# Layer norms' factors and biases on the token-major rows: from GpSimd right behind the norm to VectorE steps spread over the next part

## The chip, the cores and the metric

One NeuronCore of a Trainium2 chip runs the whole program. Time is device microseconds (us) of one execution; a kernel's time is the median of its runs. Five engines run side by side, each with a queue of its own that it works off in order: TensorE (PE in the profile) multiplies and transposes into PSUM, VectorE (DVE), ScalarE (ACT) and GpSimd (POOL) work on rows of 128 partitions, SyncE (SP) issues most loads. They wait for one another through semaphores only.

## The reference, cut to what matters

512 tokens of 1024 features pass two layers of feed-forward, token mixer, feed-forward, and then a second block with a mixer and experts. Each of the six parts of the two layers ends in a layer norm:

```python
for l in range(DEPTH):          # DEPTH = 2
    x = layer_norm(ALPHA * x + 0.5 * swiglu(x, ...), ln_f1_g[l], ln_f1_b[l])    # norm 0
    x = layer_norm(ALPHA * x + token_mixer(x, ...), ln_mix_g[l], ln_mix_b[l])   # norm 1
    x = layer_norm(ALPHA * x + 0.5 * swiglu(x, ...), ln_f2_g[l], ln_f2_b[l])    # norm 2
# layer_norm(x, g, b) = (x - mean) * rsqrt(var + eps) * g + b, over the 1024 features
```

Then `second_block(x)`: an RMS norm, three kinds of mixing, a residual, routed experts.

## The kernel before, in words

**Two forms of x.** The token-major rows are four tiles `self.x[0..3]` of 128 tokens by 1024 features in float32. The products need x feature-major and in two parts, `xh` and `xl` (high digits and the rest), as every product is made of three TensorE passes (`mm3`, lines 219 to 222). A weight is loaded, copied by ScalarE into its high part (line 204), and VectorE subtracts to get the low part (line 205); five buffers hold high parts, five low parts.

**The end of a part** is `down_ln`. The last product is made in two halves of 512 features. In the second half, tile after tile: the last products of tile t, then `ln_z` (VectorE adds the residual and takes statistics, lines 305 and 306); after every second tile `ln_finish` (mean, rsqrt by small VectorE steps, and line 316, which subtracts the mean and multiplies by the inverse deviation in place). At that point the row lacks the factor g and the bias b.

**The two ways on.** `pair_T(p)` makes the feature-major parts of a pair of tiles: 16 transposes by TensorE (line 260), ScalarE applies g and b per feature (line 270, eight instructions of 128x256), and in four chunks of 512 columns VectorE copies to `xh` (line 273) and subtracts to `xl` (line 274). The first products of the next part (`self.head`: the mixer's first projection, two feed-forward columns, or the second block's) are issued between the two pairs: they need the first 256 tokens only. The token-major rows get g and b separately, by `ln_affine` (lines 320 and 321): a multiplication by `gB` and an addition of `bB`, rows of 1024 factors and biases that are the same in all partitions and, but for the last norm, already hold the next residual's ALPHA. GpSimd does both, for each of the four tiles: 8 instructions of 128x1024 per norm. These rows are needed only as the residual at the end of the next part. After norm 0 GpSimd's queue also stores them to `xs` (line 370), because the mixer's attention uses the x buffers as scratch; they come back at line 802.

**The last norm** (layer 1, norm 2; `ln_last`) is followed by the second block. There the rows are squared soon, for the RMS norm's factors (`rms`). `affine(0)` is issued ahead of `pair_T(1)`, `affine(1)` behind it; VectorE takes one tile of the four, GpSimd three.

**The order** of instructions on each engine is set when the program is built, by a scheduler that works with estimated durations; within what data allows, an instruction that comes earlier in the program goes first. `tc.issue_after(i)` places an instruction behind i on i's engine, with no wait.

**The next parts.** The feed-forward (`ffn`) goes over 22 columns f: two weights, 48 products of 128x512, an activation, and a split of the result into `hh` and `hl`. The mixer begins with four projections over the four tiles (`proj_tm` with `out_a`, `out_c`, `out_d`, `out_q`), whose results VectorE rotates (`rope`, lines 445 to 448) and ScalarE copies; `out_d` is woven with the queries and keys of the latent branch.

Of the kernel before, what the change touches and what calls it, by code (L numbers as in the profile page):

```python
# [24 lines left out]
NEG = -1e30  # L25
MLA_SCALE = 96.0 ** -0.5

# column offsets of the constant tables
# [4 lines left out]
# column offsets of the feature-major parameters of a layer  # L33
# [6 lines left out]
# the second block's tables, parameters and rows  # L40
# [15 lines left out]
def bc(ap, axis, n):  # L56
    """A view with a new axis of n equal entries."""
    shape = list(ap.shape)
    return ap.unsqueeze(axis).to_broadcast(shape[:axis] + [n] + shape[axis:])
# [7 lines left out]
def rotate(*steps):  # L67
    """The steps of several parts in turn."""
# [9 lines left out]
def weave(main, side, rate):  # L78
    """Runs main's steps, with rate steps of side to each."""
    due = 0.0  # L80
    for _ in main:
        due += rate
        while due >= 1.0:
            due -= 1.0
            next(side, None)


class Unit:
    """One head's causal attention (to one set of keys)."""
# [30 lines left out]
    def products(self, j, out, start, stop):  # L120
        """out += (vh, vl)^T ph and vh^T pl for the keys of tile j: the two halves' sum is v^T p."""
# [10 lines left out]
class DiffUnit(Unit):  # L132
    """One head's difference of two attentions."""
# [27 lines left out]
class Build:  # L161
    def __init__(self, ctx, tc, a):
# [15 lines left out]
        self.heads, self.head = [], None  # L178
        self.ident = self.const.tile([128, 128], F32, name="ident")
# [7 lines left out]
        # keep where q - k >= 0, else NEG  # L187
# [13 lines left out]
    def split(self, hi, lo, src, eng=None):  # L201
        """hi + lo = src, each with the digits that one pass of the tensor engine carries."""
        nc = self.nc
        first = nc.scalar.activation(hi, src, AF.Copy)  # L204
        (eng or nc.vector).tensor_tensor(lo, src, hi.bitcast(F32), ALU.subtract)  # L205
# [18 lines left out]
    def rsqrt(self, out, src, scale, eps):  # L224
        """out = (scale * src + eps) ** -0.5: a first guess from the exponent's bits, then three steps of Newton's."""
# [22 lines left out]
    def pair_T(self, p, g=None, b=None):  # L248
        """Feature-major parts of tokens 256 p .. 256 p + 255 of self.x (affine in the features if g)."""
# [3 lines left out]
        for cc in range(ND // 2):  # L253
# [20 lines left out]
            nc.vector.tensor_tensor(lo, f3, hi.bitcast(F32), ALU.subtract)  # L274
# [48 lines left out]
    def down_ln(self, nk, lhs, src, l, idx, coef, tail):  # L323
        """x = layer_norm(x + coef * (lhs @ w)), lhs in feature-major parts of nk chunks; src[half, pair] the weight."""
# [4 lines left out]
        if self.ln_last:  # L329
            # the gains of the next norm with these; its factors follow at the products  # L330
            for x in gb:
                self.nc.vector.tensor_tensor(x, x, self.par2[:, Q_MIXG:Q_MIXG + 8], ALU.mult)
        for half in range(2):
# [15 lines left out]
            for t in range(NT):  # L349
# [6 lines left out]
                if half == 1 and t > 1:  # L356
                    if t == 3:
                        if self.heads:
                            self.head = self.heads.pop(0)()
                        if self.ln_last:  # L360
                            self.affine(0)
                    self.pair_T(t - 2, *gb)
        if self.ln_last:
            self.affine(1)
            self.rsx = self.rms(0, 2) + self.rms(2, 2)
            return
        for t in range(NT):
            self.ln_affine(t, self.nc.gpsimd)
            if idx == 0:
                self.nc.gpsimd.dma_start(self.xs[t * 128:t * 128 + 128, :], self.x[t])  # L370

    def affine(self, p):
        for k in range(2):
            self.ln_affine(2 * p + k, self.nc.vector if (p, k) == (1, 0) else self.nc.gpsimd)

    def rms(self, t, n):
        """The factors of rms_norm(x) for the tokens of n tiles."""
# [17 lines left out]
    def ffn_head(self, l, which):  # L395
        """What can be done with the first half of the tokens, while the others are still normalised."""
# [1538 lines left out]
```

## Time and profile before

| | us |
|---|---|
| median of 3 runs (3039.59 to 3042.96) | 3039.92 |
| span of the profiled execution | 3047.0 |
| TensorE busy | 2876.3 |
| VectorE busy | 1694.6 |
| ScalarE busy | 1190.5 |
| GpSimd busy | 467.8 |

The profile is of one execution; its span is 7 us (0.2%) above the median, and the durations below are read from it. Idle and busy times of an engine in a stretch, and TensorE's granted clock there (1.00 is 2.4 GHz, 0.50 is 1.2 GHz), come from the view by stretches; the order of instructions from the timeline of one engine; in brackets behind an instruction stands how long its engine had been idle and what ended that.

### The profile page before, as it was taken

Reading aid. Unit: us, or ns where it says so; the run is one execution under the profiler, and the core shown is the slowest. Engines: PE = TensorE matmul, PEld = TensorE weight load, DVE = VectorE, ACT = ScalarE, POOL = GpSimd, SP = SyncE. Lnnn points to the kernel's source line nnn. Section 1 sums busy time; section 2 is a strip of 40 time slices with the busy share of each in tenths; the row PEclk is TensorE's granted clock in tenths of the full one; section 3 lists DMA queues with packets and bytes.
Section 4 is the critical chain, followed back from the end, with each engine's and each line's share of the span. In section 5 each row is a group of like instructions: output and inputs, shape, how many; then the busy total and the mean of one; then the engine's idle time right before and its main releaser. Section 6 shows DMA issues by size and latency. Waiting matters only on the chain. (4 is left out here: it accounts for less than half of the span.)

```text
span 3047.0 us, 38290 instructions
## 1 busy us (share of the span) xinstructions
PE 2876.3 (94%) x14451; PEld 2325.8 (76%) x14451; DVE 1694.6 (56%) x3183; ACT 1190.5 (39%) x2173; POOL 467.8 (15%) x432
## 2 busy tenths in 40 slices
PE   8999989999989999899998999998999988799787
PEld 7888878777778888788886877777888876567675
DVE  4332375877563332633326587666433258966878
ACT  3222135755432221222212475552322114255575
POOL 0000020222020000200003032202000023723334
PEclk9999989999999999899998999999999999789899
DMA  4222232112522222232223211152322212104796
GB/s 160 97 97 91 78 105 77 53 42 75 194 85 97 97 97 90 80 101 97 93 93 100 82 49 47 48 198 75 105 97 97 97 60 70 46 12 156 271 354 266
DMA packets 95554, 322.20 MB, mean 106 GB/s; under 512 B 11120, under 2 KB 11904, under 8 KB 95360
## 3 DMA queue, kind: packets, MB, share of 16 engines
q1 hardware_dynamic: 85248, 285.91, 27.5%
q0 software_dynamic: 5184, 18.88, 1.7%
q10 hardware_dynamic: 4928, 14.88, 1.4%
q8 instruction: 116, 1.90, 0.3%
q14 instruction: 78, 0.64, 0.1%
HBM read 294.98 MB, written 24.64 MB: 105 GB/s over the span
## 5 line engine op out<-in xcount | busy, mean ns | idle before, releaser
L205 DVE TENSOR_TENSOR lo<-raw,hi 128x1024 fp32r<-128x1024 f32 (+4 forms) x370 | 440.2, 1191 | 702.2 <-ACT hi L204 701.9
L204 ACT ACTIVATE hi<-raw 128x1024 fp32r<-128x1024 f32 (+4 forms) x370 | 380.1, 1032 | 1118.5 <-PE pa L221 300.8
L221 PE MATMUL pa<-xl,hi 128*128 128x512 f32 (+1 forms) x808 | 307.2, 380 | 18.6 <-DVE xl L274 18.5
L320 POOL TENSOR_TENSOR x<-x,gB 128x1024 f32<-128x1024 f32 x23 | 58.9, 2579 | 1709.1 <-PE pa L260 1528.3
L220 PE MATMUL pa<-xh,hi 128*128 128x512 f32 (+1 forms) x808 | 307.3, 381 | 13.1 <-DVE xh L273 13.1
L222 PE MATMUL pa<-xh,lo 128*128 128x512 f32 (+1 forms) x808 | 305.2, 378 | 0.0
L221 PE MATMUL pb<-xl,hi 128*128 128x512 f32 (+1 forms) x784 | 292.3, 373 | 0.0
L220 PE MATMUL pb<-xh,hi 128*128 128x512 f32 (+1 forms) x784 | 291.9, 373 | 0.0
L222 PE MATMUL pb<-xh,lo 128*128 128x512 f32 (+1 forms) x784 | 291.9, 372 | 0.0
L417 DVE TENSOR_TENSOR sg<-sg,pb 128x512 f32<-128x512 f32 x88 | 60.5, 688 | 284.4 <-PE pb L222 276.4
L221 PEld LDWEIGHTS pa<-xl,hi 128*128 128x128 f32 x808 | 156.2, 193 | 48.6 <-DVE xl L274 21.8
L220 PEld LDWEIGHTS pa<-xh,hi 128*128 128x128 f32 x808 | 156.3, 193 | 43.3 <-DVE xh L273 16.1
L222 PE MATMUL pa<-hi,xl 128*128 128x512 f32 (+4 forms) x416 | 158.6, 383 | 22.7 <-DVE xl L274 22.7
L220 PE MATMUL pa<-hi,xh 128*128 128x512 f32 (+4 forms) x416 | 164.9, 399 | 13.0 <-DVE xh L273 10.1
L222 PEld LDWEIGHTS pa<-xh,lo 128*128 128x128 f32 x808 | 156.8, 194 | 26.4
L221 PEld LDWEIGHTS pb<-xl,hi 128*128 128x128 f32 x784 | 150.5, 192 | 25.0
L220 PEld LDWEIGHTS pb<-xh,hi 128*128 128x128 f32 x784 | 150.2, 192 | 25.0
L222 PEld LDWEIGHTS pb<-xh,lo 128*128 128x128 f32 x784 | 150.1, 191 | 24.9
L220 PE MATMUL pa<-hi,hh 128*128 128x512 f32 x416 | 165.8, 399 | 1.5 <-ACT hh L204 1.5
L221 PE MATMUL pa<-lo,xh 128*128 128x512 f32 (+4 forms) x416 | 157.5, 379 | 9.4 <-DVE lo L205 9.4
L221 PE MATMUL pa<-lo,hh 128*128 128x512 f32 x416 | 164.7, 396 | 0.1
L222 PE MATMUL pa<-hi,hl 128*128 128x512 f32 x416 | 164.5, 395 | 0.0
(550 smaller groups left out, 6284.4 us busy)
## 6 DMA issues: line engine op xcount, KB each, us to landing
raw<-in_gu SPq DMA_DIRECT2D x176, 512.0 KB, 3.3
raw<-in_wd SPq DMA_DIRECT2D x88, 512.0 KB, 3.3
mraw<-in_eg SPq DMA_DIRECT2D x51, 512.0 KB, 8.4
raw<-in_win_g SPq DMA_DIRECT2D x32, 512.0 KB, 3.2
mraw<-in_ed SPq DMA_DIRECT2D x20, 512.0 KB, 5.3
sig<-sg SPq DMA_DIRECT2D x32, 256.0 KB, 2.0
raw<-in_wp SPq DMA_DIRECT2D x16, 512.0 KB, 4.4
sg<-sig SPq DMA_DIRECT2D x32, 256.0 KB, 3.4
```

The source lines that it names most:

```text
L204: first = nc.scalar.activation(hi, src, AF.Copy)
L205: (eng or nc.vector).tensor_tensor(lo, src, hi.bitcast(F32), ALU.subtract)
L220: nc.tensor.matmul(out, sh, mh, start=start, stop=False)
L221: nc.tensor.matmul(out, sh, ml, start=False, stop=False)
L222: nc.tensor.matmul(out, sl, mh, start=False, stop=stop)
L320: eng.tensor_tensor(self.x[t], self.x[t], self.gB, ALU.mult)
L417: nc.vector.tensor_tensor(sg, sg, pu, ALU.mult)
```

## The change

The factor and bias of a norm leave GpSimd and the end of the part. For five of the six norms they become a sequence of eight VectorE steps (`late_affine`: for each tile the multiplication, then the addition). The mixer takes one step at the end of each `out_c` and one inside each `out_d`; the feed-forward takes one step per column from f = 4 on. What is left is run before the fourth projection, or before the feed-forward's `down_ln`. Each step is placed behind `self.pin`, the VectorE instruction that the program issued last among the subtractions of `split` and `pair_T` and the last sums of `rope`. The stores to `xs` after norm 0 stay in GpSimd's queue and follow their tile's addition. For the last norm, each `pair_T` is followed at once by the four VectorE instructions of its two tiles, placed behind the pair's last subtraction.

```diff
     def split(self, hi, lo, src, eng=None):
         first = nc.scalar.activation(hi, src, AF.Copy)
-        (eng or nc.vector).tensor_tensor(lo, src, hi.bitcast(F32), ALU.subtract)
+        last = (eng or nc.vector).tensor_tensor(lo, src, hi.bitcast(F32), ALU.subtract)
+        if eng is None:
+            self.pin = last
...
@@ pair_T
-            nc.vector.tensor_tensor(lo, f3, hi.bitcast(F32), ALU.subtract)
+            self.pin = nc.vector.tensor_tensor(lo, f3, hi.bitcast(F32), ALU.subtract)
...
@@ down_ln
                 if half == 1 and t > 1:
-                    if t == 3:
-                        if self.heads:
-                            self.head = self.heads.pop(0)()
-                        if self.ln_last:
-                            self.affine(0)
+                    if t == 3 and self.heads:
+                        self.head = self.heads.pop(0)()
                     self.pair_T(t - 2, *gb)
+                    if self.ln_last:
+                        with self.tc.issue_after(self.pin.ins):
+                            for k in range(2):
+                                self.ln_affine(2 * t - 4 + k, self.nc.vector)
         if self.ln_last:
-            self.affine(1)
             self.rsx = self.rms(0, 2) + self.rms(2, 2)
             return
+        self.late = self.late_affine(self.x, self.gB, self.bB, idx == 0)
+
+    def late_affine(self, x, g, b, store):
+        nc = self.nc
         for t in range(NT):
-            self.ln_affine(t, self.nc.gpsimd)
-            if idx == 0:
-                self.nc.gpsimd.dma_start(self.xs[t * 128:t * 128 + 128, :], self.x[t])
+            for y, op in ((g, ALU.mult), (b, ALU.add)):
+                with self.tc.issue_after(self.pin.ins):
+                    nc.vector.tensor_tensor(x[t], x[t], y, op)
+                if store and op == ALU.add:
+                    nc.gpsimd.dma_start(self.xs[t * 128:t * 128 + 128, :], x[t])
+                yield
...
@@ ffn, in the loop over f and behind it
                 act(f, pg, pu)
+                if f > 3:
+                    next(self.late, None)
+            run(self.late)
@@ rope
-        nc.vector.tensor_tensor(dst, t1, t2, ALU.add)
+        self.pin = nc.vector.tensor_tensor(dst, t1, t2, ALU.add)
@@ mixer_, out_c (at its end) and out_d (behind its rope)
+            next(self.late, None)
@@ mixer_, before the fourth projection
+        run(self.late)
```

## Rows read from the trace of the kernel before

**Rows 1.** Page, part 1: busy time, share of the span and instructions of each engine

```profile
PE 2876.3 (94%) x14451; PEld 2325.8 (76%) x14451; DVE 1694.6 (56%) x3183; ACT 1190.5 (39%) x2173; POOL 467.8 (15%) x432
```

**Rows 2.** Waits of TensorE, whole span: who waited for whom, total us, times, longest

```profile
PE pa L220 <- DVE xh L273: 23.2, 22, 1.7
PE pa L222 <- DVE xl L274: 22.7, 11, 5.1
...
PE pa L221 <- DVE xl L274: 18.5, 10, 2.4
```

**Rows 3.** VectorE's timeline, first norm, first pair: start, us, engine, line, operation

```profile
377.97 2.60 DVE L273 CAST xh<-full 128x512 fp32r<-128x512 f32 x1
380.61 2.74 DVE L274 TENSOR_TENSOR xl<-full,xh 128x512 fp32r<-128x512 f32 x1
...
388.54 0.45 DVE L273 CAST xh<-full 128x512 fp32r<-128x512 f32 x1
389.03 0.69 DVE L274 TENSOR_TENSOR xl<-full,xh 128x512 fp32r<-128x512 f32 x1
```

**Rows 4.** GpSimd's timeline in the same stretch; each row merges two instructions

```profile
377.90 4.90 POOL L320 TENSOR_TENSOR x<-x,gB 128x1024 f32<-128x1024 f32 x2 [376.25 <-PE pa L260]
382.75 5.32 POOL L321 TENSOR_TENSOR x<-x,bB 128x1024 f32<-128x1024 f32 x2
```

**Rows 5.** By stretches: from:to, length, busy PE, PEld, DVE, ACT, POOL, clock, DMA

```profile
376.00:400.00 24.00, 17.92 (x71) 14.51 (x70) 21.67 (x33) 6.25 (x11) 11.74 (x10) 0.79 0.45 152
400.00:424.00 24.00, 18.18 (x80) 14.85 (x79) 17.44 (x28) 8.70 (x20) 11.62 (x6) 0.79 0.16 56
848.00:870.00 22.00, 18.00 (x110) 16.02 (x109) 21.15 (x30) 7.26 (x12) 10.58 (x4) 0.92 0.14 49
872.00:894.00 22.00, 15.65 (x101) 14.30 (x100) 14.88 (x11) 7.77 (x13) 10.53 (x4) 0.77 0.23 83
1236.00:1258.00 22.00, 16.26 (x101) 14.82 (x99) 20.93 (x29) 6.44 (x11) 10.15 (x4) 0.84 0.14 48
1260.00:1282.00 22.00, 16.11 (x92) 14.67 (x90) 15.19 (x13) 7.94 (x13) 10.52 (x4) 0.69 0.15 52
1622.00:1646.00 24.00, 17.96 (x71) 14.58 (x72) 21.97 (x33) 6.25 (x11) 11.57 (x10) 0.79 0.47 151
1646.00:1670.00 24.00, 18.20 (x81) 14.87 (x80) 17.43 (x28) 8.70 (x20) 11.59 (x6) 0.79 0.16 56
2099.00:2119.00 20.00, 16.63 (x94) 14.76 (x92) 19.38 (x27) 6.11 (x10) 10.46 (x4) 0.83 0.16 53
2123.00:2143.00 20.00, 13.64 (x85) 12.29 (x84) 13.94 (x10) 7.38 (x13) 10.53 (x4) 0.74 0.23 79
2484.00:2508.00 24.00, 16.90 (x95) 14.98 (x94) 22.91 (x33) 6.01 (x11) 13.01 (x9) 0.79 0.24 73
2508.00:2528.00 20.00, 14.52 (x105) 14.06 (x104) 16.57 (x40) 11.00 (x21) 5.59 (x2) 0.83 0.08 26
```

**Rows 6.** TensorE's timeline: the first product of the mixer's head

```profile
381.20 0.37 PE L220 MATMUL pa<-hi,xh 128*128 128x440 f32 x1
```

**Rows 7.** The one addition of a bias that VectorE makes today, by its line

```profile
L321 DVE TENSOR_TENSOR x<-x,bB x1: 1211/1211/1211, 2519.5 to 2519.5; 128x1024 f32<-128x1024 f32 x1
```

**Rows 8.** By stretches: a feed-forward, and the mixer's third and fourth projection

```profile
910.00:1110.00 200.00, 200.00 (x884) 165.62 (x883) 68.11 (x74) 57.54 (x73) 0.00 (x0) 1.00 0.29 98
464.00:480.00 16.00, 15.46 (x91) 13.65 (x90) 14.27 (x44) 13.40 (x29) 0.00 (x0) 1.00 0.25 82
```

**Rows 9.** VectorE's timeline in the mixer, behind the second projection

```profile
459.21 0.96 DVE L205 TENSOR_TENSOR lo<-raw,hi 128x768 fp32r<-128x768 f32 x1 [8.74 <-ACT hi L204]
```

**Rows 10.** ScalarE's timeline: the attention's first write to a buffer of x

```profile
511.27 0.37 ACT L493 ACTIVATE pr<-pa,sm 128x128 f32<-128x128 f32 x1
```

**Rows 11.** GpSimd's and VectorE's timelines behind the last norm's first pair

```profile
2496.86 2.07 POOL L1184 MEMSET sc<- 128x2048 f32 x1
...
2497.23 0.69 DVE L274 TENSOR_TENSOR xl<-full,xh 128x512 fp32r<-128x512 f32 x1
2497.84 1.38 DVE L273 CAST xh<-full 128x512 fp32r<-128x512 f32 x1
```

More of the change, by code (lines that the diff above doesn't have):

```diff
@@ L178, in __init__ @@
         self.heads, self.head = [], None
+        self.late = iter(())
         self.ident = self.const.tile([128, 128], F32, name="ident")
@@ L356, in down_ln @@
                 if half == 1 and t > 1:
-                    if t == 3:
-                        if self.heads:
-                            self.head = self.heads.pop(0)()
-                        if self.ln_last:
-                            self.affine(0)
+                    if t == 3 and self.heads:
+                        self.head = self.heads.pop(0)()
                     self.pair_T(t - 2, *gb)
+                    if self.ln_last:
+                        with self.tc.issue_after(self.pin.ins):
+                            for k in range(2):
+                                self.ln_affine(2 * t - 4 + k, self.nc.vector)
         if self.ln_last:
-            self.affine(1)
             self.rsx = self.rms(0, 2) + self.rms(2, 2)
             return
+        self.late = self.late_affine(self.x, self.gB, self.bB, idx == 0)
+    def late_affine(self, x, g, b, store):
+        nc = self.nc
         for t in range(NT):
-            self.ln_affine(t, self.nc.gpsimd)
-            if idx == 0:
-                self.nc.gpsimd.dma_start(self.xs[t * 128:t * 128 + 128, :], self.x[t])
-    def affine(self, p):
-        for k in range(2):
-            self.ln_affine(2 * p + k, self.nc.vector if (p, k) == (1, 0) else self.nc.gpsimd)
+            for y, op in ((g, ALU.mult), (b, ALU.add)):
[4 more added lines that the diff above has]
+                yield
     def rms(self, t, n):
@@ L634, in out_d @@
             self.rope(ksw[1][:, t, :, :16], v[:, 1, :, :16], 2, 8, tab(C_NCOS, t, 16), tab(C_NSIN, t, 16))
+            next(self.late, None)
             nc.scalar.activation(ksw[1][:, t, :, 16:], v[:, 1, :, 16:], AF.Copy)
```

## The prediction

> **What bounds the kernel now.** I read the page first: TensorE is busy for 2876.3 of 3047.0 us [rows 1], so what counts is what stops it. The list of its waits comes next. Three lines at its top name one place, the copy and the subtraction that make `xh` and `xl` behind a norm: 23.2 + 22.7 + 18.5 = 64.4 us [rows 2]. Six norms have two pairs of tiles each, so that is some 5.4 us a pair. Third, the timelines of VectorE and GpSimd side by side. In the first pair of the first norm a copy takes 2.60 us and a subtraction 2.74 [rows 3]; in the same pair, once GpSimd has finished at 388.07, they take 0.45 and 0.69 [rows 3, 4]. The long ones start and end with GpSimd's instructions of 2.45 to 2.66 us (4.90 and 5.32 for two) [rows 4]: each VectorE instruction waits until one of GpSimd's is through, then does its own work. Without them a chunk costs 0.45 + 0.69 = 1.14 us instead of 2.60 + 2.74 = 5.34. GpSimd's four instructions hold up two chunks in each pair, so the price is 2 x 4.2 = 8.4 us of VectorE time per pair, on TensorE's path.
>
> The Trainium skill states this as a lock (SBUF — State Buffer, section "SBUF: two separate sides"): VectorE and GpSimd share a pair of ports, the first to start keeps it for its whole instruction, and a VectorE instruction with two SBUF inputs is held only by a GpSimd instruction that reads SBUF. The rows agree, and I use the second half of the rule below.
>
> **What the stalls cost in full.** Fourth, the stretches. Behind every pair TensorE's granted clock falls from its higher level (2.4 GHz) to the lower (1.2 GHz), after it has stood idle for some of the time; the means over such a stretch are 0.69 to 0.92 [rows 5]. What a stretch loses is its length less busy time times clock. For the first pairs of the six norms: 24 - 17.92 x 0.79 = 9.8, and likewise 5.4, 8.3, 9.8, 6.2, 10.7; for the second pairs 9.6, 10.0, 10.9, 9.6, 9.9, 8.0 [rows 5]. Sum: 50.2 + 58.0 = 108.2 us. Of it 268.0 - 200.0 = 68.0 is idle time and 40.2 the slower clock, so a microsecond of such stalls has cost 108.2 / 68.0 = 1.59. The 108.2 are the most that this place can give.
>
> **Removed: 46 GpSimd instructions and their lock.** Not all of the 108.2 returns, since the chain behind the norm remains. First pairs: VectorE starts at 377.97 [rows 3], and at 1.14 us a chunk would be done at 382.5; TensorE arrives at 381.20 [rows 6], when two chunks are ready, and needs the rest one after the other. So a wait of 0 to 1.3 us remains; then come the subtractions of the head's last weights, which VectorE now reaches 8 us earlier. Second pairs: nothing lies between the transposes and the products that need them; TensorE waits for the first chunk and then follows at about VectorE's pace, 0.4 to 2.3 us (a first copy, to half of 4 x 1.14). I take 1 us for each of the 12 pairs, near the middle of both bounds: 12 us remain, 96.2 return, the clock's part with them, because I expect no idle time above 1 us in one piece. Bounds: 80 (2.3 us for each of 12) to 106.
>
> **Added: 46 VectorE instructions of 1.21 us** (the addition that VectorE makes today takes 1211 ns [rows 7]), 55.7 us, at three kinds of place.
>
> *Feed-forward, 3 x 8 steps, 29 us.* VectorE is busy for 68.11 of 200 us there, and TensorE for 200.00 at full clock [rows 8]. A step stands at a column's end, behind its last subtraction; queued behind it are the next weights' subtractions, which run several weights ahead of the products, and the next activation. The cover is VectorE's idle 66%. Cost 0; 29 if the cover were gone. A new wait: the next norm's factors overwrite `gB` and `bB`, so their loads, in ScalarE's queue, now wait for the last of the eight steps; ScalarE's weight copies queue behind, with as much lead. Cost 0, too: those rows are used only a hundred or more us later.
>
> *Mixers, 2 x 8 steps, 9.7 us each.* Here VectorE is not free. Four steps stand in `out_c`. The other four are placed behind the rotations of `out_d`, and VectorE comes to these only after a subtraction for which it stood idle for 8.74 us, at 459.21 [rows 9]: the steps cannot use that gap and land in 464 to 480, where VectorE is busy for 14.27 of 16 us and TensorE already loses 0.54 [rows 8]. Behind each of these steps queue the rotations, the weights' subtractions and the compression's inputs, and TensorE waits for them. There is room for 1.73 us; 4 x 1.21 = 4.84 come. So 3.1 us stick out, and I add 0.4 for the first four: 3.5 a mixer, 7 us in all. Bounds: 0 (the scheduler orders around them) to 2 x 9.7 = 19.4. The `xs` stores move with the additions in GpSimd's queue, which has nothing else to do there; the attention's first write to a buffer of x is at 511.27 [rows 10], some 30 us after the last step. Cost 0.
>
> *Last norm, 8 instructions where VectorE had 2.* Four follow the first pair at once: 4.84 us on VectorE ahead of the head weights' subtractions, of `ln_z` and of the second pair's norm, all of which TensorE needs soon. GpSimd's memsets (the longest 2.07 us [rows 11]), which stand behind its affine instructions today, may come earlier and meet this pair. Cost 5 us, between 0 (ordered behind the urgent ones) and 4.84 + 2.07 = 6.9. In today's trace a memset let a subtraction pass at 0.69 and held a copy for about 1 us (1.38) [rows 11]. By the skill's rule on instructions that read SBUF (same section) a memset could hold only the copies, as these rows have it; by that the upper end stays 6.9. Behind the second pair TensorE has two tiles' products and half a column's, so 1.5 of the 4.84 us, between 0 and 4.84. Together 6.5.
>
> **The sum.** 108.2 - 12 - 7 - 6.5 = 82.7 us. Against the profiled span: 3047.0 - 82.7 = 2964. The median lies 7.1 us (0.23%) below that span, so 3039.9 - 82.7 = 2957 us.
>
> **Rivals.**
> 1. *Everything is hidden.* The scheduler places all steps in gaps, and half a microsecond remains per pair: 108.2 - 6 = 102, 2938 us. For it: VectorE is idle for 44% of the span [rows 1]. Against: the program's order goes first, and the mixer's steps are behind busy rotations.
> 2. *VectorE becomes the bound where the steps stand close.* All 16 steps of the mixers reach TensorE, with the clock: 19.4 x 1.59 = 31; the last norm's first pair returns nothing (9.7) and its second loses 4.8: 108.2 - 12 - 31 - 14.5 = 51, 2989 us. For it: 14.27 of 16 [rows 8]. Against: TensorE has products in store from other branches there.
> 3. *The clock falls anyhow*, at the smaller gaps and the transposes. Only idle time returns: 68.0 - 12 - 13.5 = 42.5, 2997 us. Against: the clock was 1.00 in 464 to 480 with 0.54 us idle [rows 8].
> 4. *Every step stops TensorE (the slower side).* Place: the split behind each step, in feed-forward, mixer and last norm. Price: 48 x 1.21 x 1.59 = 92 against 96 returned, 3036 us; from 2.0 us a step (96 / 48) it is slower, at 2.2 by 9 us, 3049. Against: 200.00 of 200 with a VectorE two thirds idle [rows 8].
> 5. *The change does not do what it says:* the long copies are not GpSimd's doing. Nothing returns, 13.5 are added: 3053 us. Against: 2.60 and 0.45 within one pair, on either side of 388.07 [rows 3, 4].
>
> **How the numbers follow.** Forecast 0.62 (its own range 2945 to 2975: mixers 0 to 14, remainders 6 to 18), rival 1 0.13, rival 2 0.13, rival 3 0.07, rival 4 0.03, rival 5 0.02. Predicted is 2957. The range runs from 2937, which takes in rival 1, to 2989, which takes in rival 2; outside are rivals 3 to 5 and strays, below 2 in 10. A measurement of this kernel tells 0.2% (6 us) from no change: faster is the forecast with rivals 1 to 3, 0.95; same is a part of rival 4, 0.02; slower the rest, 0.03.
>
> **What would show it.** In the trace after: copies at about 0.45 and subtractions at 0.69 behind every norm, no GpSimd instruction beside them; the three waits of [rows 2] from 64 us down to about 10; the clock at 1.00 through the stretches of [rows 5], but for the last norm's; lines of 1.21 us on VectorE in the feed-forwards with TensorE still without a wait; in the mixers new TensorE waits of 2 to 4 us for rotations or weights' low parts after the second projection. It would be wrong if the waits for `xl` stay at 2 us a piece (rivals 3, 5), if the mixers lose more than 10 us (rival 2), or if the feed-forward shows any TensorE wait (rival 4).

## The result and the profile after

| | before | after |
|---|---|---|
| median, us | 3041.44 (3039.59 to 3045.24, 4 runs) | 2956.49 (2947.45 to 2959.41, 4 runs) |
| ratio, 95% interval | | 0.9709 [0.9691, 0.9727] |
| span of the profiled execution, us | 3047.0 | 2945.7 |
| VectorE busy, us | 1694.6 | 1647.5 |
| GpSimd busy, us | 467.8 | 349.0 |

The change makes the kernel 85 us (2.9%) faster. The profiled execution of after is the shortest of its four and that of before lies above all of its runs, so the two pages are 101 us apart. Where a few us matter below, several profiled executions stand side by side.

**VectorE got 46 instructions more and is busy for less time.** Part 1 of the page after answers to [rows 1]: busy time, share of the span, instructions.

```profile
PE 2831.6 (96%) x14451; PEld 2294.7 (78%) x14451; DVE 1647.5 (56%) x3229; ACT 1192.5 (40%) x2174; POOL 349.0 (12%) x386
```

The new instructions add 46 x 1.22 = 56 us and the sum still falls by 47: about 103 us of VectorE's busy time before were time in which an instruction was held, not worked on. VectorE's timeline after, first norm, first pair, answers to [rows 3]:

```profile
377.71 0.43 DVE L276 CAST xh<-full 128x512 fp32r<-128x512 f32 x1
378.18 0.69 DVE L277 TENSOR_TENSOR xl<-full,xh 128x512 fp32r<-128x512 f32 x1
378.79 0.42 DVE L276 CAST xh<-full 128x512 fp32r<-128x512 f32 x1
379.24 0.69 DVE L277 TENSOR_TENSOR xl<-full,xh 128x512 fp32r<-128x512 f32 x1
379.85 0.42 DVE L276 CAST xh<-full 128x512 fp32r<-128x512 f32 x1
```

The first copy took 2.60 us before and takes 0.43, the first subtraction 2.74 and 0.69. Of the 48 copies behind the norms the longest is now 0.46. TensorE's waits after (who waited for whom, total, times, longest) answer to [rows 2]:

```profile
PE pb L1224 <- DVE lvB L1211: 14.6, 3, 11.4
PE pb L1224 <- DVE sm L235: 9.3, 1, 9.3
...
PE pb L1014 <- DVE sm L1013: 4.2, 1, 4.2
...
PE pa L223 <- DVE xh L276: 2.5, 6, 0.7
```

Of the three lines with 64.4 us one is left, with 2.5. The two that lead the list now belong to the second block (`L1224` was `L1210`); they come up again below. The stretches behind the norms, and a feed-forward and a piece of a mixer at the end, answer to [rows 5] and [rows 8]; from:to, length, busy PE, PEld, DVE, ACT, POOL, clock, DMA:

```profile
376.00:391.00 15.00, 14.96 (x79) 13.11 (x77) 13.04 (x33) 6.26 (x11) 0.35 (x4) 1.00 0.52 173
391.00:414.00 23.00, 21.83 (x120) 19.64 (x121) 17.40 (x66) 10.79 (x29) 0.00 (x0) 1.00 0.23 69
829.00:848.00 19.00, 19.00 (x139) 17.89 (x138) 14.96 (x31) 7.77 (x12) 0.00 (x0) 1.00 0.33 111
848.00:868.00 20.00, 19.69 (x140) 18.29 (x139) 11.60 (x16) 12.25 (x18) 0.00 (x0) 1.00 0.32 104
...
2389.00:2408.00 19.00, 16.18 (x112) 14.30 (x110) 17.82 (x37) 5.91 (x11) 2.87 (x5) 1.00 0.33 95
2408.00:2428.00 20.00, 15.05 (x100) 13.89 (x99) 17.85 (x48) 14.02 (x25) 0.00 (x0) 0.83 0.20 64
886.00:1086.00 200.00, 200.00 (x883) 165.48 (x882) 76.88 (x81) 59.63 (x75) 0.00 (x0) 1.00 0.32 103
440.00:460.00 20.00, 19.91 (x114) 17.56 (x113) 18.31 (x55) 14.91 (x31) 0.53 (x1) 1.00 0.39 132
```

Behind five norms TensorE's clock stays at its higher level (1.00), and the ten pairs together lose 3.3 us (the four of the first two norms 0.04, 1.17, 0 and 0.31). In the feed-forward VectorE's busy time rose from 68.11 to 76.88, and TensorE is still busy for 200.00 of 200. Only the last norm still loses time: 19 - 16.18 = 2.8 and 20 - 15.05 x 0.83 = 7.5 us.

**Where the time came from, part by part.** From the first copy behind one norm to the first copy behind the next, each read from VectorE's timeline; the last column goes to the end of the span. `same_again` and `third_look` are further executions of the changed kernel, `before_again` is one of the kernel before.

| us from norm to norm | 0 to 1 (mixer) | 1 to 2 (ffn) | 2 to 3 (ffn) | 3 to 4 (mixer) | 4 to 5 (ffn) | 5 to end |
|---|---|---|---|---|---|---|
| before | 472.1 | 386.6 | 387.6 | 475.1 | 386.6 | 560.9 |
| before_again | 470.3 | 386.8 | 387.6 | 471.1 | 387.0 | 556.5 |
| after | 453.0 | 370.7 | 368.4 | 450.5 | 370.8 | 554.6 |
| same_again | 455.3 | 370.7 | 368.4 | 454.4 | 370.7 | 559.7 |
| third_look | 450.9 | 370.7 | 368.4 | 451.4 | 370.7 | 563.0 |
| saved, of means | 18.1 | 16.0 | 19.2 | 21.0 | 16.1 | -0.4 |
| lost before by [rows 5] | 19.4 | 15.4 | 19.2 | 19.4 | 16.1 | 18.7 |

The first five columns give back what [rows 5] says was lost there: 90.4 against 89.5. By the stretches alone it would be 86.2, as 3.3 us are still lost in them; the other 4 us lie mostly in the second mixer's column, whose executions spread by as much. The sixth column gives back nothing that shows in a spread of 8 us. That is the finding which the experiments had to explain.

### The profile page after: what moved, and what is told of

The parts are those of the page before. It is cut to its first block, busy times and chain, and to the rows that moved or that the text cites. A ratio compares the mean times of both kernels' runs of the same rounds, so it can differ in the third digit from the quotient of the medians.

```text
span 2945.7 us, 38251 instructions
## 1 busy us (share of the span) xinstructions
PE 2831.6 (96%) x14451; PEld 2294.7 (78%) x14451; DVE 1647.5 (56%) x3229; ACT 1192.5 (40%) x2174; POOL 349.0 (12%) x386
## 5 line engine op out<-in xcount | busy, mean ns | idle before, releaser
L225 PEld LDWEIGHTS pb<-xh,lo 128*128 128x128 f32 x784 | 147.8, 189 | 25.5 <-DVE lo L206 0.4
L224 PEld LDWEIGHTS pb<-xl,hi 128*128 128x128 f32 x784 | 147.6, 188 | 24.9
L223 PE MATMUL pa<-hi,xh 128*128 128x512 f32 (+4 forms) x416 | 155.9, 377 | 2.7 <-DVE xh L276 1.5
L224 PE MATMUL pa<-lo,xh 128*128 128x512 f32 (+4 forms) x416 | 151.1, 364 | 6.4 <-DVE lo L206 6.3
L225 PE MATMUL pa<-hi,xl 128*128 128x512 f32 (+4 forms) x416 | 149.3, 361 | 0.0
```

The source lines that it names most:

```text
L223: nc.tensor.matmul(out, sh, mh, start=start, stop=False)
L224: nc.tensor.matmul(out, sh, ml, start=False, stop=False)
L225: nc.tensor.matmul(out, sl, mh, start=False, stop=stop)
```

## The experiments

My theory was the prediction's: GpSimd's instructions hold VectorE's, so the place of the work counts, and the steps cost next to nothing where they stand. The rivals were that the gain comes from the faster engine, or from the work as such, and that the last norm's eight instructions take back more than counted.

**same_again and third_look: the changed kernel again**, for the spread and as neighbours of the others on their chips.

> The changed kernel once more, for a second profiled execution. The changed kernel's four runs lay between 2947.5 and 2959.4 us, with mean granted clocks of 0.974 down to 0.968. If the difference between its executions is the clock in parts that the change does not touch (attention, second block), this execution shows the same intervals from norm to norm within 1 us in the feed-forwards, and differs only where the clock is below 1.00 without idle time. If it comes from the moved steps, the intervals of feed-forward or mixer differ.

> The changed kernel beside the three others of this call, on the same chip: 2950 to 2959 us, and a third profiled execution. From norm to norm its feed-forwards take 352 us again; the stretches with attention and the second block differ by up to 5 us each, with the clock.

Measured: 2954.15 us, 0.9703 [0.9683, 0.9722], and 2953.89 us, 0.97 [0.9686, 0.9714]. The feed-forwards repeat to 0.1 us, the mixers and the second block do not (table above). The 352 us of the second expectation and of a later one, and the 361 to 363 for the kernel before, are counted from a norm's second pair on: 370.7 - 18.8 = 351.9.

**no_affine: what the 48 instructions cost where they now stand.**

```diff
@@ down_ln
                     if self.ln_last:
-                        with self.tc.issue_after(self.pin.ins):
-                            for k in range(2):
-                                self.ln_affine(2 * t - 4 + k, self.nc.vector)
+                        pass
@@ late_affine
-                with self.tc.issue_after(self.pin.ins):
-                    nc.vector.tensor_tensor(x[t], x[t], y, op)
```

> Leaves out the token-major rows' factors and biases altogether (all 48 instructions; the stores stay where they are), so its difference from the changed kernel is the price of the 48 VectorE instructions. Theory (the 40 steps in the next parts are free, the 8 behind the last norm are not): the changed kernel's profile has 2.9 us of TensorE idle time in the last norm's first pair and 7.3 us of idle and slow clock in its second, so some 9 us: 2947 us against 2956. Rival (the steps also cost TensorE time in mixer and feed-forward, 3.5 us a mixer and more): 2940 or less. Second rival (nothing costs anything): within 3 us of 2956.

Measured: 2945.81 us, 0.9679 [0.966, 0.9698], some 8 us below the changed kernel beside it. The five parts up to the last norm's first copy take 2017.9 us (378.04 to 2395.95) against 2013.3, 2019.5 and 2012.2 in the three executions of the table, with the same feed-forwards to 0.1 us: the 40 steps cost nothing that shows. From the last norm to the end it takes 546.9 against 554.6 to 563.0. What the change costs, it costs behind the last norm, with the eight instructions there.

**right_behind: VectorE does the work, but at once behind each pair, at every norm.**

```diff
-                    if self.ln_last:
-                        with self.tc.issue_after(self.pin.ins):
-                            for k in range(2):
-                                self.ln_affine(2 * t - 4 + k, self.nc.vector)
+                    with self.tc.issue_after(self.pin.ins):
+                        for k in range(2):
+                            self.ln_affine(2 * t - 4 + k, self.nc.vector)
+                    if idx == 0:
+                        for u in (2 * t - 4, 2 * t - 3):
+                            self.nc.gpsimd.dma_start(self.xs[u * 128:u * 128 + 128, :], self.x[u])
...
-        self.late = self.late_affine(self.x, self.gB, self.bB, idx == 0)
```

> VectorE does the multiplication and addition of both tiles right behind each pair's last subtraction, for all six norms, as the changed kernel does for the last one only; GpSimd has none of them. Theory (engine and place both count: no lock, but 4.84 us of VectorE work between the pair and what TensorE needs next): each of the ten pairs that change loses about what the last norm's first pair loses today, 2.9 us, so some 29 us: about 2985 us; copies stay at 0.43 us. Rival (only the engine counts, the place is indifferent): 2956. Other rival (only the place counts, work right behind the norm costs the same whoever does it): about 3040.

Measured: 2973.98 us, 0.9772 [0.9756, 0.9788]: 18 to 20 us above the changed kernel. So VectorE in GpSimd's stead gives most of the gain (68 of 88 us), although its work still stands at the norm, and the later place gives the rest, less than the 29 us I expected. (The place is not quite GpSimd's: VectorE's four instructions come behind the pair's last subtraction, GpSimd's ran beside the copies.) VectorE's timeline behind the first pair, and a TensorE wait that comes of it:

```profile
382.03 2.35 DVE L323 TENSOR_TENSOR x<-x,gB 128x1024 f32<-128x1024 f32 x2
384.30 2.35 DVE L324 TENSOR_TENSOR x<-x,bB 128x1024 f32<-128x1024 f32 x2
387.18 1.06 DVE L206 TENSOR_TENSOR lo<-raw,hi 128x880 fp32r<-128x880 f32 x1
```

```profile
388.29 0.47 PE L224 MATMUL pa<-lo,xh 128*128 128x440 f32 x1 [2.37 <-DVE lo L206]
```

The first of these splits of the head's weights starts 9.9 us behind the first copy, against 5.3 in the changed kernel, and TensorE waits 2.4 us for the low part.

**no_pin: the same steps without the fixed point behind `self.pin`.**

```diff
-                with self.tc.issue_after(self.pin.ins):
-                    nc.vector.tensor_tensor(x[t], x[t], y, op)
+                nc.vector.tensor_tensor(x[t], x[t], y, op)
```

> The changed kernel with the 40 late steps placed by program order alone, without the fixed point behind the last subtraction or rotation. Theory (the scheduler takes what is ready: the rows and factors are ready at the norm, so the steps go into VectorE's first gaps, between the norm and the first rotations): the steps move forward into the stretch right behind the pairs, and the time lies near the kernel that does them there, 2965 to 2975 us. Rival (program order keeps them late, the fixed point changes nothing): 2955.

Measured: 2975.07 us, 0.9777 [0.9762, 0.9792], as much as `right_behind`. The scheduler moves the steps forward, since their data are ready; its VectorE timeline:

```profile
378.00 1.23 DVE L377 TENSOR_TENSOR x<-x,gB 128x1024 f32<-128x1024 f32 x1
379.14 0.76 DVE L276 CAST xh<-full 128x512 fp32r<-128x512 f32 x2
...
390.49 1.22 DVE L377 TENSOR_TENSOR x<-x,bB 128x1024 f32<-128x1024 f32 x1
```

The first step stands ahead of the first copy, although the program has it a mixer's projection later. Writing a step later in the program does not place it; the 20 us of the later place come from the line that fixes it.

**pool_late: GpSimd does the work at the late places.** A copy of one column (`o`) of what `self.pin` wrote was meant to hold GpSimd back until then.

```diff
-                with self.tc.issue_after(self.pin.ins):
-                    nc.vector.tensor_tensor(x[t], x[t], y, op)
...
+                nc.gpsimd.tensor_copy(self.seen, o)
+                nc.gpsimd.tensor_tensor(x[t], x[t], y, op)
```

> GpSimd does the late steps at the changed kernel's places in feed-forward and mixer (a small copy of one column of the result that VectorE has just written, about 0.15 us, holds GpSimd until that point); the last norm is as in the changed kernel. Theory (a VectorE instruction meeting one of GpSimd's waits up to 2.6 us, and that costs only where VectorE has no lead): feed-forwards as in the changed kernel, no TensorE wait; in the mixers, where VectorE is busy for 18.3 of 20 us, each of the 8 steps holds it for up to 2.6 us, up to 20 us a mixer: between 2960 and 2990 us. Rival (GpSimd's work costs wherever it runs): about 3040. Second rival (place is all): 2956.

Measured: 3038.58 us, 0.9978 [0.9966, 0.9991]. The experiment did not do what it was to do, as GpSimd's timeline shows:

```profile
377.95 4.90 POOL L383 TENSOR_TENSOR x<-x,gB 128x1024 f32<-128x1024 f32 x2 [376.30 <-PE pa L264]
382.81 5.32 POOL L383 TENSOR_TENSOR x<-x,bB 128x1024 f32<-128x1024 f32 x2
...
437.69 0.19 POOL L382 COPY seen<-ks 128x1 f32<-128x1 f32 x1 [24.75 <-DVE ks L463]
```

Only the copies were held; the scheduler took the work itself ahead of them, back to its old place (compare [rows 4]). It tells nothing of late GpSimd steps. It shows by accident that the changed program with GpSimd right behind the five norms has nearly the old time.

**pool_held: the same, with each step placed behind its copy.**

```diff
-                nc.gpsimd.tensor_copy(self.seen, o)
-                nc.gpsimd.tensor_tensor(x[t], x[t], y, op)
+                seen = nc.gpsimd.tensor_copy(self.seen, o)
+                with self.tc.issue_after(seen.ins):
+                    nc.gpsimd.tensor_tensor(x[t], x[t], y, op)
```

> As the run before it with GpSimd's late steps (there the scheduler had moved GpSimd's instructions back to right behind the norm, since only VectorE's queue had a fixed point), but each multiplication and addition is now placed behind the small copy that holds GpSimd at the changed kernel's place. Theory (the harm is VectorE meeting GpSimd where it has no lead): feed-forward intervals of 352 us as in the changed kernel, tails without a stall, mixers up to 20 us longer each: 2960 to 2990 us. Rival (GpSimd's work costs wherever it runs): about 3040.

Measured: 2963.82 us, 0.9743 [0.9728, 0.9758]. The slow engine at a good place is within 10 us of the changed kernel, better than the fast engine right behind the norm (2974). From norm to norm it takes 456.4, 370.7, 368.4, 457.3 and 370.7: the feed-forwards are those of the changed kernel to 0.1 us, and the mixers lose some 3 and 5. Why, the timelines of GpSimd and VectorE in the first mixer show:

```profile
419.99 2.40 POOL L384 TENSOR_TENSOR x<-x,gB 128x1024 f32<-128x1024 f32 x1
...
432.33 2.41 POOL L384 TENSOR_TENSOR x<-x,gB 128x1024 f32<-128x1024 f32 x1
```

```profile
419.58 0.19 DVE L464 TENSOR_TENSOR ks<-r,r 128x32 f32<-128x32 f32 x1
...
420.09 2.34 DVE L464 TENSOR_TENSOR kc_tm<-r,r 128x32 f32<-128x32 f32 x1
...
432.21 2.59 DVE L464 TENSOR_TENSOR kc_tm<-r,r 128x32 f32<-128x32 f32 x1
```

A sum of 32 columns that takes 0.19 us takes 2.34 and 2.59 beside GpSimd's multiplications and ends within 0.1 us of them. (The second is recorded as starting 0.12 us ahead of GpSimd's; so close a start doesn't settle which came first.) TensorE is busy for 18.09 of the 20 us from 440 on, where the changed kernel has 19.91. This is the hold of [rows 3] at another place and on another instruction; in a feed-forward GpSimd's step of 2.4 us falls into 3.6 us in which VectorE is idle.

**half_pool: the kernel before without the additions of the biases.** Half of GpSimd's work goes; the place and the engine stay.

```diff
         eng.tensor_tensor(self.x[t], self.x[t], self.gB, ALU.mult)
-        eng.tensor_tensor(self.x[t], self.x[t], self.bB, ALU.add)
```

> The kernel before, leaving out the biases' additions on the token-major rows (line 321, 24 instructions), so that GpSimd has two instructions behind each pair instead of four. Theory (each of GpSimd's instructions holds one of VectorE's for its rest): one chunk of each pair is held instead of two, 4.2 us less per pair on VectorE; TensorE's stall falls from some 9 us a pair to 3 or 4, the more as shorter gaps may leave the clock at its upper level: 2970 to 2995 us. Rival (the copies and subtractions are slow for another reason): 3040, with copies still at 2.6 us in two chunks of each pair.

Measured: 2994.57 us, 0.9851 [0.9829, 0.9874], 48 us below the kernel before beside it (3042.94): half the hold gives a little over half of the 85 to 91 us. VectorE and GpSimd in its first pair:

```profile
377.66 2.62 DVE L273 CAST xh<-full 128x512 fp32r<-128x512 f32 x1
380.31 2.74 DVE L274 TENSOR_TENSOR xl<-full,xh 128x512 fp32r<-128x512 f32 x1
382.97 0.46 DVE L273 CAST xh<-full 128x512 fp32r<-128x512 f32 x1
383.47 0.69 DVE L274 TENSOR_TENSOR xl<-full,xh 128x512 fp32r<-128x512 f32 x1
```

```profile
377.59 4.91 POOL L320 TENSOR_TENSOR x<-x,gB 128x1024 f32<-128x1024 f32 x2 [375.95 <-PE pa L260]
```

Two GpSimd instructions hold two of VectorE's, one chunk; the second chunk is short as soon as GpSimd has ended (377.59 + 4.91 = 382.50). In the kernel before it was held too, here its copy:

```profile
383.27 2.59 DVE L273 CAST xh<-full 128x512 fp32r<-128x512 f32 x1
```

So it is GpSimd's instructions that hold VectorE, one by one, which settles rival 5. The Trainium skill's rule (SBUF — State Buffer, "SBUF: two separate sides"), that the loser of the shared pair of ports waits for the other's whole instruction, agrees with these rows and with those of `pool_held`.

**last_as_before: the changed kernel, but the last norm as it was** (`affine(0)` ahead of `pair_T(1)`, `affine(1)` behind it; three tiles by GpSimd).

```diff
...
+                        if self.ln_last:
+                            self.affine(0)
                     self.pair_T(t - 2, *gb)
-                    if self.ln_last:
-                        with self.tc.issue_after(self.pin.ins):
-                            for k in range(2):
-                                self.ln_affine(2 * t - 4 + k, self.nc.vector)
         if self.ln_last:
+            self.affine(1)
...
```

> The changed kernel with the last norm's rows as in the kernel before (GpSimd three tiles, VectorE one). Theory (the last norm gave 6.7 us from its first to its second pair and about nothing behind, since the second pair's stall of 5 us became a wait of 4.2 us for the factors): 6 to 8 us slower than the changed kernel, 2960 to 2964 us; first to second pair 24.9 us again. Rival (the last norm gave the 10 us that were predicted for it): 2965 or more.

Measured: 2955.53 us, 0.9709 [0.9696, 0.9722], against 2953.89 for the changed kernel beside it. My expectation was wrong: with the last norm undone, the time is the same within the intervals. The hold is back, as its VectorE timeline and its stretch show, and still it costs nothing at the end:

```profile
2395.18 2.61 DVE L276 CAST xh<-full 128x512 fp32r<-128x512 f32 x1
```

```profile
2394.00:2418.00 24.00, 16.35 (x85) 14.32 (x84) 22.89 (x32) 6.01 (x11) 12.75 (x9) 0.72 0.23 75
2418.00:2440.00 22.00, 16.52 (x115) 15.84 (x114) 17.21 (x42) 11.59 (x22) 5.59 (x2) 0.84 0.12 42
```

These two lose 12.2 and 8.1 us, the changed kernel's two 2.8 and 7.5: a gain of 10 behind the norm. How far it lasts is seen on VectorE's timeline further on, as time since the last norm's first copy:

| us since the first copy | first scan of decays | first norm of the convolution (`sq`) | last level's sum (`acc`) | end |
|---|---|---|---|---|
| before, before_again | 58.2, 58.6 | 84.8, 85.2 | 201.0, 201.2 | 560.9, 556.5 |
| last_as_before | 59.7 | 88.0 | 200.9 | 558.4 |
| after, same_again, third_look | 48.4, 48.8, 48.3 | 80.5, 80.9, 81.9 | 197.6, 197.6, 198.7 | 554.6, 559.7, 563.0 |
| half_pool | 52.7 | 79.3 | 193.9 | 553.8 |
| no_affine | 41.7 | 68.4 | 182.9 | 546.9 |

A gain of 10 us at the scan is 4 at the convolution's norm and 3 at the last level, and then is lost in a spread of 8 us between executions of one kernel. It need not be so: `half_pool` and `no_affine` come to the scan 6 and 17 us earlier than the kernel before and to the last level 7 and 18 us earlier. From the scan to the last level's sum, by stretches, before, after and `no_affine`:

```profile
2544.00:2688.00 144.00, 116.03 (x1277) 88.01 (x1276) 128.91 (x286) 38.45 (x59) 81.21 (x62) 0.87 0.16 49
2439.00:2589.00 150.00, 118.01 (x1285) 89.67 (x1285) 129.65 (x285) 41.46 (x61) 79.78 (x62) 0.89 0.14 43
2437.00:2579.00 142.00, 115.77 (x1272) 86.88 (x1271) 127.62 (x283) 38.49 (x59) 81.79 (x62) 0.89 0.16 49
```

After takes 6 us longer than before. VectorE is busy there for 0.7 us more and idle for 20.4 us instead of 15.1; most of the added idle time is waits for TensorE ahead of the levels' sums (`tm`: 9.7 us instead of 6.3). And the work has another order: between the scan and the convolution's norm VectorE does eight steps of the convolution's sum (`y<-z,par,y`) in all executions of the changed kernel, and four in `before`, `last_as_before`, `half_pool` and `no_affine`. Inside this stretch lies a piece in which VectorE and GpSimd are both busy almost throughout, first of before, then of after:

```profile
2576.00:2636.00 60.00, 38.66 (x390) 27.96 (x389) 59.77 (x107) 10.12 (x17) 60.00 (x48) 0.77 0.11 36
```

```profile
2481.00:2541.00 60.00, 32.18 (x351) 23.10 (x349) 59.87 (x106) 10.48 (x18) 58.45 (x47) 0.77 0.11 36
```

VectorE is busy for 59.8 of 60 us, GpSimd for 58.5 to 60 and TensorE for 32 to 39: in this piece TensorE is not the bound. VectorE's and GpSimd's timelines in it, of after:

```profile
2481.53 0.15 DVE L237 SCALAR_TENSOR_TENSOR sm<-sm 128x8 f32<-128x8 f32 x1
2481.65 1.07 DVE L1055 SCALAR_TENSOR_TENSOR y<-z,par,y 128x512 f32<-128x512 f32 x1
2482.64 1.22 DVE L235 TENSOR_TENSOR sm<-sm 128x8 f32<-128x8 f32 x1
```

```profile
2482.15 1.69 POOL L1058 TENSOR_TENSOR y<-y,zw 128x512 f32<-128x512 f32 x1
```

An instruction on 8 columns takes 0.15 us or 1.22, and the long one ends (2483.86) with GpSimd's (2483.84). It is the same hold, in a part whose instructions the change doesn't touch. But it doesn't explain the lost gain: before has the same piece, and so has `no_affine`, whose 17 us come through it. Where the changed kernel loses its 10 us is read from the landmarks; that the other order is the reason is not shown, as no run changed the order alone.

**last_later: the last norm's first four instructions behind the head's last weight split.**

```diff
+                        if self.ln_last:
+                            with self.tc.issue_after(self.pin.ins):
+                                for k in range(2):
+                                    self.ln_affine(k, self.nc.vector)
                     self.pair_T(t - 2, *gb)
-                    if self.ln_last:
+                    if self.ln_last and t == 3:
                         with self.tc.issue_after(self.pin.ins):
                             for k in range(2):
-                                self.ln_affine(2 * t - 4 + k, self.nc.vector)
+                                self.ln_affine(2 + k, self.nc.vector)
```

> The changed kernel with the last norm's first four VectorE instructions behind the head's last weight split instead of right behind the pair. Theory (these 4.84 us held up the head's weights, ln_z and the second pair's norm, 2.9 us of TensorE idle time): TensorE's waits between the last norm's first and second pair fall from 2.9 us to under 1 us, and the time by 2 to 3 us, 2953 us. Rival (the four are late for the second pair instead, and its squares): the second pair's stall of 4.2 us for the factors grows by as much; no change. The time alone will hardly tell it, as executions spread over 12 us; the profile does.

Measured: 2952.04 us, 0.9704 [0.969, 0.9717]: 2 to 4 us below the changed kernel's medians, with a ratio that isn't to be told from theirs. First to second pair takes 17.6 us instead of 18.2. TensorE's idle time in between falls from 2.98 to 2.49 us only, not under 1 as I expected, and the wait of 4.2 us for the factors stays. The place of these four matters little.

**k_first: on top of `last_later`, the keys' products go ahead of what needs the RMS factors.** Behind the second pair TensorE waited 4.2 us for the factors (`L1014` above), whose rows wait for the four instructions on VectorE. The keys' products need only `xh` and `xl`.

```diff
...
+        kk = self.proj_fm(a["w2_fm"][1], scaled(k, 1.0), self.pb)
+        for _ in range(ND - 1):
+            next(kk)
         for t in range(NT):
             out_v(t, pre[t])
         spread()
...
-        run(self.proj_fm(a["w2_fm"][1], scaled(k, 1.0)))
+        run(kk)
```

> The changed kernel with the last norm's first four instructions behind the head's weights, and the products of the linear attention's keys issued ahead of the steps that need the RMS factors (in a free bank), so that TensorE has 5.6 us of work while VectorE and ScalarE make these factors. Theory (behind the second pair TensorE waits 4.2 us for the factors, and the clock falls): that wait falls below 1 us, the clock stays at its upper level there, 4 to 6 us less than the changed kernel with the later four instructions, 2946 to 2949 us, near the kernel without any of these rows. Rival (the wait moves to the next step that needs the factors, or the weights' low part comes too late): 2952.

Measured: 2941.99 us (2940.07 to 2949.08), 0.9664 [0.9651, 0.9678], against 0.97 [0.9686, 0.9714] for the changed kernel beside it: 10 us below `last_later`, where I expected 4 to 6; 12 us faster than the change, 103 us faster than before, and the best version here. The stretch behind the second pair:

```profile
2410.00:2430.00 20.00, 19.25 (x125) 16.38 (x124) 18.38 (x50) 14.06 (x26) 0.00 (x0) 1.00 0.21 65
```

The 4.2-us wait is gone and the clock holds: 0.75 us lost, where the changed kernel loses 7.5. Here half of the 12 us shows up to the levels: their last sum comes 191.3 us after the first copy, where the changed kernel's comes after 197.6 to 198.7 and that of `last_later` after 195.6. The other half of the 12 us I can't place: from that sum to the end it takes 362.9 us, within the 357 to 364 of the others.

**before_again: one look at the kernel before**, beside the changed one.

> The kernel before once more, for a second profiled execution: feed-forwards of 361 to 363 us and tails of 25 us from the first to the second pair within 0.5 us of the first execution; the mixers and the second block up to 5 us different, with the clock. If so, the norms' share of the difference is the same in any pair of executions, and the rest is the clock's.

Measured: 3038.32 us; its intervals stand in the table above. From first to second pair it takes 24.8 to 25.5 us, in the first execution 24.9 to 25.5.

## Why the prediction was right, point by point

Predicted 2957 us, between 2937 and 2989; measured 2956.5. At the first five norms the mechanism is the forecast's. The sum, 82.7 us against a measured 85 to 91, fits because two errors of its terms have opposite signs; that the number came out within 1 us is luck.

**The place and its price: right.** 108.2 us were lost behind the norms, 89.5 of it behind the first five, and these give back 90.4 by the table, the slower clock's share with them. Rival 3, by which only idle time returns, is out: the clock is 1.00 in the ten stretches. Rival 5 is out by `half_pool`.

**What remains of the chain, 12 us: too much.** The ten pairs of the first five norms lose 3.3 us, not 10. In first pairs TensorE arrives when chunks are ready and VectorE keeps ahead of it (0.04 lost of 15 us behind the first norm); I had taken the middle of my bounds where the lower end holds. Second pairs lose 0.3 to 1.2.

**The mixers' steps, 7 us: too much; they cost nothing that shows.** The steps do land where I put them, beside busy rotations:

```profile
444.39 1.22 DVE L378 TENSOR_TENSOR x<-x,gB 128x1024 f32<-128x1024 f32 x1
...
448.85 1.22 DVE L378 TENSOR_TENSOR x<-x,bB 128x1024 f32<-128x1024 f32 x1
...
457.21 1.22 DVE L378 TENSOR_TENSOR x<-x,gB 128x1024 f32<-128x1024 f32 x1
...
461.93 1.22 DVE L378 TENSOR_TENSOR x<-x,bB 128x1024 f32<-128x1024 f32 x1
```

This is VectorE's timeline after. The four are spread over 18.8 us, where I had packed them into 16, and TensorE shows no wait above 0.13 us from 416 to 470; from 440 to 460 it is busy for 19.91 of 20 beside a VectorE busy for 18.31. The failing step is "There is room for 1.73 us; 4 x 1.21 = 4.84 come": VectorE's free time was counted as TensorE's reserve. TensorE had products of another branch to do, as I wrote against rival 2 and did not price. `no_affine` agrees: without the steps the five parts take as long, within the 4 us by which the mixers differ between executions.

**The feed-forward's steps, 0: right.** 200.00 of 200 busy, intervals of 370.7 and 368.4 that repeat to 0.1 us. VectorE stands idle for 2.48 us behind each step.

**The last norm: right in its place, wrong in what follows.** I let 18.7 of loss return less 2 of remainder and 6.5 of steps, 10.2 us. Behind the norm that is about what happened: 2.8 + 7.5 = 10.3 us of 18.7 are still lost there, and the scan comes 10 us earlier. The failing step is that I asked what is late next only as far as the pair, and let the whole gain there count at the end: in the next 150 us the second block, in another order, takes 6 to 7 us longer, and by the end nothing of the 10 is left that shows (-0.4 in the table; `last_as_before`). Within the place the sizes were off both ways: the first pair lost 2.8, where I had 6 (1 and 5), the second 7.5, where I had 2.5. There the four instructions delay the RMS rows and so the factors, which I had not followed; `k_first` shows that this wait was worth going round.

So: five norms 90.4 where I had 89.5 - 10 - 7 = 72.5, the last norm about 0 where I had 10.2. Rival 1 was nearer for the five norms than the forecast, and missed the last one as I did.

**GpSimd's memsets: no harm.** They did come earlier, as feared; GpSimd's and VectorE's timelines after:

```profile
2395.41 1.81 POOL L1198 MEMSET sc<- 128x2048 f32 x1
```

```profile
2395.85 2.35 DVE L323 TENSOR_TENSOR x<-x,gB 128x1024 f32<-128x1024 f32 x2
```

Two multiplications beside the memset take 2.35 us, as the two additions at 2398.12 do without one. The Trainium skill's rule (SBUF — State Buffer, "SBUF: two separate sides"), that an instruction with two SBUF inputs is held only by a GpSimd instruction that reads SBUF, agrees.

**What stays open.** From the last level's sum to the end the three executions of the changed kernel took 357.0 to 364.3 us and those with the last norm as before 355.3 to 359.9; whether another us or two is given back there can't be told from these. Why the last norm's gain is lost in the second block stays open: how much VectorE's six additional instructions account for, and how much the other order of its work, wasn't separated. TensorE's wait of 9.3 us for `sm` is not in the list before, but it isn't the answer, as `last_as_before`, `half_pool` and `no_affine` have it too (9.3 to 9.8 us).

## What to carry to other kernels

When a cheap instruction shows two lengths in one timeline, lay the other engine's timeline beside it: if the long ones end where that engine's instructions end, move the other engine's work out of the stretch. Here that returned nearly the whole loss behind five norms (86 of 89.5 us), the clock's part too, and the engine that then did the work mattered less than the place (2964 us for GpSimd at late places, 2974 for VectorE at the norm). A step that is written later is placed later only if something fixes it there (`no_pin`, `pool_late`), so check in the trace where it ran. And follow each gain to the end by landmarks: 10 us behind the last norm were 3 us 150 us later in the changed kernel, while other versions carried theirs through.

## What the runs showed of the hardware

- The clock's fall is not in proportion to the idle time of the same stretch. In `half_pool` the first stretch has TensorE busy for 18.10 of 24 us at a clock of 1.00 and the second for 21.82 of 24 at 0.86; before, the same first stretch had 17.92 busy at 0.79 [rows 5]. My 1.59 us per idle us was a ratio of this one trace, no rate. Stretches, as above:

```profile
376.00:400.00 24.00, 18.10 (x97) 15.33 (x96) 20.50 (x35) 9.12 (x18) 9.69 (x10) 1.00 0.45 152
400.00:424.00 24.00, 21.82 (x103) 19.32 (x104) 18.44 (x64) 8.30 (x24) 3.13 (x3) 0.86 0.33 110
```

- What differs between executions of one kernel lies in the parts with the mixers and in the second block, not in the feed-forwards: 450.9 to 455.3, 450.5 to 454.4 and 554.6 to 563.0 us against 370.7 and 368.4 each time. The mean granted clock differs with it: the four runs after, 2947.45, 2953.96, 2959.03 and 2959.41 us, had 0.974, 0.971, 0.968 and 0.968.
- A held instruction's length is about the holder's, not its own: a sum of 32 columns (0.19 us alone) and a copy of 512 (0.42) both took 2.3 to 2.6 us beside a GpSimd instruction of 2.4 to 2.7.
